# Ten of eleven FFN pairs as groups, first sums by transfer, and a tail by token tiles

## The chip, the cores and the metric

The kernel runs on one core of a Trainium2 chip. The metric is the device time of one execution in microseconds; the kernel before stands at 2078.82 us, the median of three runs (2076.89 to 2081.77).

## The reference

One layer of a macaron block on 256 tokens, model width 2048, in fp32: half a SwiGLU FFN, two token mixers side by side, a second half FFN and a last RMSNorm.

```python
x = x + 0.5 * swiglu_ffn(rmsnorm(x, norm_ffn1_g[l]), ffn1_w_gate[l], ffn1_w_up[l], ffn1_w_down[l])
h = rmsnorm(x, norm_mix_g[l])
proj = h @ w_in[l]
...
merged = jax.nn.sigmoid(gate_a) * branch_a + jax.nn.sigmoid(gate_r) * branch_r
x = x + merged @ w_out[l]
x = x + 0.5 * swiglu_ffn(rmsnorm(x, norm_ffn2_g[l]), ffn2_w_gate[l], ffn2_w_up[l], ffn2_w_down[l])
return rmsnorm(x, norm_final_g)
```

where `swiglu_ffn` is `(silu(x @ w_gate) * (x @ w_up)) @ w_down` with an inner width of 5632. branch_a is band attention over 8 heads with a clipped relative-position bias, branch_r is chunkwise retention over 8 heads.

## The kernel before

**One product.** Each fp32 operand is split into a high and a low part, and a product is three matmuls: high by high, low by high, high by low (L132, L133, L135; `three`). The weights are split on the fly: ACT copies a 128x1024 tile to the high part (L123), VectorE subtracts it from the raw tile for the low part (L124; `split`).

**Standard steps.** A `Gemm` has an output of 256 tokens by 512 columns in two PSUM banks. Its step takes 256 rows of the weight: a load by SP (L117), a split, and 12 matmuls of 128x512.

**Groups.** The inner width is 11 blocks of 512 columns. For each block the gate and the up product are needed: a *pair*. As two `Gemm`s a pair has 16 standard steps, 192 matmuls. As a *group* (class `Strassen`) the two products are built by seven block products in place of eight, 28 steps of six matmuls, 168 in all. Its phases, with jc = 0..3:
- phase 0, r: split of k[jc] (bank a); VectorE also makes the first sum x[jc] = x[jc] + k[jc] (L505). Phase 0, s: split of that x[jc] (bank c).
- phase 1, r: a raw weight tile, split (bank c); VectorE adds it to x[jc] (L560). Phase 1, s: split of x[jc] (bank a); VectorE makes k[jc] = x[jc] - k[jc] (L547), and an accumulating transfer on POOL adds another part of the up weight to x[jc] (L548, the third sum).
- phase 2, r: a raw tile (bank b). Phase 2, s: k[jc] (bank a). Phase 3, s: x[jc] (bank a).

r and s alternate, so 10r names phase 1, jc 0, r. Between phases a bank is read by ACT: a after 03r into b (L600), c after 03s (L603), a after 13s and after 23s (L617); VectorE joins the partial results (L733 and its neighbours), ACT applies silu. Then TensorE transposes the block (f1a4p is block 4 of FFN 1), and its halves are split for the down product (`put`, L353 and L354). The operands k and x of the next group are eight POOL loads of 512 KB (L516), each issued when a tile of an earlier group is free. The mixing stage has five groups of the same kind.

**The order.** An FFN makes some of the blocks as plain pairs (`PLAIN`) and the rest as groups. The down product runs in passes (`PASSES`), each over one or two blocks as four `Gemm`s, whose accumulators ACT seeds with the running sum (L750) and evicts to it (L753). `weave` writes the order of all steps down: it lays the group's steps in order and puts a standard step after a pair of them when a credit, fed by the table `SHARE`, allows and the standard step's blocks are at hand (`at_hand`, a fixed number of steps after the last step of the block). Preparation (load, split) runs up to four steps ahead of the products (four split buffers). `later(n)` puts work n steps further on.

**Tail.** The last down block's two steps (`TAIL` = 2) run by token tile and column part; the last norm's scaling and the stores of both token tiles stand at the end (`scale_rows`).

**The code.** The functions that the change touches, with the profile's line numbers:

Of the kernel before, what the change touches and what calls it, by code (L numbers as in the profile page):

```python
# [11 lines left out]
ALU = mybir.AluOpType  # L12
# [3 lines left out]
P = 128  # L16
SEQ = 256
NT = SEQ // P
# [14 lines left out]
SPLIT_BUFS = 4  # L33
KEPT = 8
ACT_TILES = 30
TAIL = 2
AHEAD = (2, 3)
HALF_K = D // P // 2
LEAD = 12
# [1 line left out]
RET_WAIT = (14, 5)  # L41
HELD = 6

SHARE = (0.85,) * 4 + (1.0,) * 4 + (0.8,) + (0.4,) * 3 + (0.15,) * 4
PLAIN = (9, 10)
PASSES = ((9, 0), (1, 2), (10, 3), (4, 5), (6,), (7,), (8,))
GATE_WAIT = 5
WARM = (6, 3)
TAIL_PARTS = ((0, slice(0, NB)), (1, slice(0, NB // 2)), (1, slice(NB // 2, NB)))

# [22 lines left out]
def block_kernel(ctx: ExitStack, tc: tile.TileContext, x, g1, w1g, w1u, w1d, gm, w_in, rel, woa, wor, wo,  # L73
# [156 lines left out]

    def run(tail_done):
        head = len(steps) - TAIL
        last = steps[-1].job
        last.parts = TAIL_PARTS
# [12 lines left out]
        for part, (t, cs) in enumerate(TAIL_PARTS):  # L247
            for c in range(head, len(steps)):
                steps[c].products(part)
            tail_done(last.acc[part], t, cs)  # L250
        while due:
            s = min(due)
            state["step"] = max(s, state["step"])
            for fn in due.pop(s):
                fn()
# [73 lines left out]
    def bias_natural(bt):  # L329
        for b in range(HEADS // 4):  # L330
            table["bias", b] = act_tile(F32, f"bias{b}")
        for h in range(0, HEADS, 2):
            ps = side_tile(f"psb{h}")
            for i in range(2):
                for j in range(2):
                    nc.tensor.transpose(
                        ps[:, (2 * i + j) * P : (2 * i + j + 1) * P],
                        bt[(h + i) // 4][:, (h + i) % 4, j * P : (j + 1) * P],
                        id_sb,
                    )  # L340
            nc.scalar.copy(table["bias", h // 4][:, h % 4 : h % 4 + 2, :].rearrange("p h k -> p (h k)"), ps)
        for b in range(HEADS // 4):
            nc.vector.memset(table["bias", b][0:CHUNK, :, CHUNK:P], MASKED)


    def rsqrt(dst, ssum, n, width):
# [143 lines left out]
    class Strassen:  # L490
# [19 lines left out]

        def loads(self):


            def go(tiles, i, jc):
                tiles[jc] = apool.tile([P, KC, NB], F32, tag="act", name=f"{self.name}{'kx'[i]}{jc}")
                nc.gpsimd.dma_start(tiles[jc], chunk(self.w[i], self.rows(0, jc), self.col[i]))  # L516

            return [
                lambda tiles=tiles, i=i, jc=jc: go(tiles, i, jc)
                for jc in range(HALF_K // KC) for i, tiles in enumerate((self.kept, self.x))  # L520
            ]

        def steps(self):
# [10 lines left out]
        def step(self, phase, jc, of_sum):  # L534
# [15 lines left out]
            def prep():  # L550
                x = self.x[jc]
                if not of_sum:
                    if phase == 0:
                        made["w"] = split(self.kept[jc], name)
                        self.first(jc)
                        return
                    raw = made.pop("raw")
                    made["w"] = split(raw, name)
                    if phase == 1:
                        nc.vector.tensor_add(x, x, raw)  # L560
                elif phase == 2:
# [85 lines left out]
    def weave(jobs, apart, groups, lead, start=None):  # L647
# [17 lines left out]

        for _ in range(lead):
# [4 lines left out]
        for n, (b, make) in enumerate(groups.items()):  # L671
# [15 lines left out]
    def ffn(name, norm, wg, wu, wd, after, start=None):  # L687
# [10 lines left out]
        def plain(b):  # L698
# [15 lines left out]
            def up_done(acc):  # L714
                for t in range(NT):
                    a = gates[t]
                    nc.vector.scalar_tensor_tensor(a, acc[t], norm.scale(t), a, op0=ALU.mult, op1=ALU.mult)  # L717
# [7 lines left out]
        def paired(b):  # L725
            got = {}

            def evict(t, side, r):
# [3 lines left out]
                    return  # L732
                nc.vector.scalar_tensor_tensor(got[t], r, norm.scale(t), got[t], op0=ALU.mult, op1=ALU.mult)  # L733
                if t == 1:
                    later(3, lambda: put_mid(b, got))

            return Strassen(norm, wu, b * NB, wg, b * NB, evict)

# [336 lines left out]
        for t in range(NT):  # L1075
            last_square(t, slice(b * NB, (b + 1) * NB), b)

    def tail_done(acc, t, cs):
        cols = slice(D - NB + cs.start, D - NB + cs.stop)
        xb = xs[t][:, cols]  # L1080
        part = D // NB - 1 + (cs.start > 0)
        if cs.stop == NB:
# [3 lines left out]
        nc.vector.scalar_tensor_tensor(xb, acc, 0.5, xb, op0=ALU.mult, op1=ALU.add)  # L1086
        if "end" not in fin:
            fin["end"] = tmp_tile(f"end{t}", "qk", 4)
        end = fin["end"]
        last_square(t, cols, part, end[:, cs])  # L1090
        if cs.stop < NB:
            return
        del fin["end"]
        v = small.tile([P, 1], F32, tag="v", name="v")
        nc.vector.tensor_scalar(v, nf_ss[:, t, part : part + 1], 1.0 / D, before, op0=ALU.mult, op1=ALU.add)
        rs = small.tile([P, 1], F32, tag="frs", name="frs")
        nc.gpsimd.tensor_tensor(rs, v, mhalf[:, :1], op=ALU.pow)
        fin[t] = rs, end

        if t == NT - 1:  # L1100
            for u in range(NT):
                scale_rows(u)

    def scale_rows(t):
        rs, end = fin[t]
# [137 lines left out]
```

## Time and profile before

| | |
|---|---|
| median of 3 runs | 2078.82 us (2076.89 to 2081.77) |
| profiled execution | 2078.51 us, its span 2076.4 us |
| TensorE busy | 2048.9 us, 99% of the span |
| VectorE busy | 1756.2 us, 85% |
| ScalarE busy | 1404.3 us, 68% |
| GpSimd busy | 273.7 us, 13% |
| chain that ended last | PE 92% |
| HBM read | 462.65 MB |

In the profile, PE is TensorE, DVE is VectorE, ACT is ScalarE, POOL is GpSimd, and SP issues the weight transfers. The chain is followed back from the last instruction: at each step to what released it. A name as `loz12823s` is the low part (`lo`) of the group that begins at step 128 (`z128`), phase 2, jc 3, s.

### The profile page before, as it was taken

To read this page: it belongs to the slowest core of one execution; us is meant where nothing else is said; L and a number is where in the kernel's file an instruction comes from. 1 tells how busy PE (TensorE), PEld (TensorE's weight loads), DVE (VectorE), ACT (ScalarE), POOL (GpSimd) and SP (SyncE) were. 2 spreads that over 40 slices of the span, in tenths; PEclk is the share of its full clock that TensorE was granted. 3 is DMA by queue.
4 is the path that set the end of the run, shared out by engine and by line. 5 is a ranking of instruction groups with operands and counts; after the bars stand their busy time and mean duration, and the time that the engine had idled before them with its cause. 6 is when DMAs were issued, how large, how long until landed. Compare 5 with 4: busy or idle time off the path is not lost.

```text
span 2076.4 us, 26151 instructions
## 1 busy us (share of the span) xinstructions
PE 2048.9 (99%) x9256; PEld 1692.5 (82%) x9256; DVE 1756.2 (85%) x1823; ACT 1404.3 (68%) x1734; POOL 273.7 (13%) x322
## 2 busy tenths in 40 slices
PE   9999999999999999999999999999999999999997
PEld 7788888888888888888878888888888878888886
DVE  7998899898997799898866667568889988998986
ACT  8677667777777776767665434556676677677785
POOL 1111211122111111112100000010122112210200
PEclk9999999999999999999999999999999999999999
DMA  8777886788678777789775645575788668866873
GB/s 305 210 223 232 263 238 197 239 256 260 189 229 263 242 209 242 252 273 281 226 243 173 222 137 189 186 248 165 236 270 244 187 228 264 248 197 233 274 213 132
DMA packets 219027, 473.28 MB, mean 228 GB/s; under 512 B 14784, under 2 KB 15536, under 8 KB 218896
## 3 DMA queue, kind: packets, MB, share of 16 engines
q1 hardware_dynamic: 161088, 310.42, 44.6%
q0 software_dynamic: 54752, 155.88, 27.8%
q10 hardware_dynamic: 3056, 5.32, 0.7%
q8 instruction: 72, 1.18, 0.2%
q14 instruction: 59, 0.48, 0.1%
HBM read 462.65 MB, written 8.91 MB: 227 GB/s over the span
## 4 chain that ended last, share of the span: by engine, by line
PE 92%; DVE 2%; DMA 2%; ACT 2%; issue 1%; ACTq 0%; POOLq 0%; DVEq 0%; POOL 0%
PE acc L132 17%; PE acc L135 17%; PE acc L133 17%; DMA raw<-in_ffn_w_down_dram 1%; DMA rawz53123r<-in_w_in_dram 1%; DVE lo L124 1%; ACT hi L123 0%; PE z128a L132 0%; PE z12a L135 0%; PE z128a L135 0%; PE z128a L133 0%; PE z12a L132 0%; PE z915a L135 0%; PE z418a L135 0%; PE z761a L132 0%
## 5 line engine op out<-in xcount | busy, mean ns | idle before, releaser
L124 DVE TENSOR_TENSOR lo<-raw,hi 128x1024 fp32r<-128x1024 f32 (+1 forms) x401 | 488.4, 1221 | 186.2 <-ACT hi L123 182.9
L123 ACT CAST hi<-raw 128x1024 fp32r<-128x1024 f32 (+1 forms) x401 | 418.7, 1048 | 231.1 <-PE acc L133 148.1
L753 ACT ACTIVATE xall<-acc 128x512 f32<-128x512 f32 x96 | 56.5, 589 | 9.4 <-PE acc L135 7.6
L750 ACT ACTIVATE acc<-xall 128x512 f32<-128x512 f32 x96 | 57.5, 599 | 8.0 <-DVE f2g L717 3.4
L132 PE MATMUL acc<-hi,mgh 128*128 128x512 f32 x128 | 50.2, 392 | 0.0
L133 PE MATMUL acc<-hi,mgl 128*128 128x512 f32 x128 | 49.8, 389 | 0.0
L132 PE MATMUL acc<-hi,nma00h 128*128 128x512 f32 x96 | 38.5, 401 | 0.0
L132 PE MATMUL acc<-hi,nma01h 128*128 128x512 f32 x96 | 38.4, 400 | 0.0
L133 PE MATMUL acc<-hi,nma00l 128*128 128x512 f32 x96 | 37.4, 390 | 0.0
L132 PE MATMUL acc<-hi,nma10h 128*128 128x512 f32 x96 | 37.4, 390 | 0.0
L133 PE MATMUL acc<-hi,nma01l 128*128 128x512 f32 x96 | 37.4, 390 | 0.0
L133 PE MATMUL acc<-hi,nma11l 128*128 128x512 f32 x96 | 37.4, 390 | 0.0
L133 PE MATMUL acc<-hi,nma10l 128*128 128x512 f32 x96 | 37.4, 389 | 0.0
L132 PE MATMUL acc<-hi,nma11h 128*128 128x512 f32 x96 | 37.4, 389 | 0.0
L135 PE MATMUL acc<-lo,mgh 128*128 128x512 f32 x128 | 35.5, 389 | 0.0
L135 PE MATMUL acc<-lo,nma11h 128*128 128x512 f32 x96 | 29.6, 390 | 0.0
L135 PE MATMUL acc<-lo,nma00h 128*128 128x512 f32 x96 | 29.6, 389 | 0.0
L135 PE MATMUL acc<-lo,nma01h 128*128 128x512 f32 x96 | 29.6, 389 | 0.0
L135 PE MATMUL acc<-lo,nma10h 128*128 128x512 f32 x96 | 29.6, 389 | 0.0
L135 PEld LDWEIGHTS acc<-lo,mgh 128*128 128x128 f32 x128 | 24.0, 188 | 5.0
L133 PEld LDWEIGHTS acc<-hi,mgl 128*128 128x128 f32 x128 | 24.0, 188 | 4.9
L132 PEld LDWEIGHTS acc<-hi,mgh 128*128 128x128 f32 x128 | 24.0, 188 | 4.8
(6130 smaller groups left out, 6934.6 us busy)
## 6 DMA issues: line engine op xcount, KB each, us to landing
raw<-in_ffn_w_down_dram SPq DMA_DIRECT2D x176, 512.0 KB, 6.2
raw<-in_w_in_dram SPq DMA_DIRECT2D x96, 512.0 KB, 4.4
raw<-in_ffn_w_up_dram SPq DMA_DIRECT2D x32, 512.0 KB, 10.0
raw<-in_w_out_dram SPq DMA_DIRECT2D x32, 512.0 KB, 4.4
raw<-in_ffn_w_gate_dram SPq DMA_DIRECT2D x31, 512.0 KB, 5.8
raw<-in_w_out_att_dram SPq DMA_DIRECT2D x16, 512.0 KB, 4.1
raw<-in_w_out_ret_dram SPq DMA_DIRECT2D x16, 512.0 KB, 3.8
z380x<-in_w_in_dram POOLq DMA_DIRECT2D x8, 512.0 KB, 7.5
```

Of the source, the lines that this page charges most:

```text
L123: nc.scalar.copy(hi[:, p, :], raw[:, p, :])
L124: nc.vector.tensor_sub(lo[:, p, :], raw[:, p, :], hi[:, p, :].bitcast(F32))
L132: nc.tensor.matmul(acc, ahi, whi, start=first, stop=False, **more)
L133: nc.tensor.matmul(acc, alo, whi, start=False, stop=False, **more)
L135: nc.tensor.matmul(acc, ahi, wlo, start=False, stop=last, **more)
L750: nc.scalar.activation(acc, xs[t][:, cols], AF.Copy, scale=2.0)
L753: nc.scalar.activation(xs[t][:, cols], acc, AF.Copy, scale=0.5)
```

## The change

1. One plain pair instead of two: block 9 alone is standard, block 10 becomes a group. The passes become (9), (0,1), (2,3), (4,5), (6,7), (8), (10); `SHARE`'s third and fourth entry go from 0.85 to 0.5; blocks count as at hand one step later; the transposes of a block come a step later (`later(4)`).
2. The first sums of jc 2 and 3 of every group are accumulating POOL transfers (`BY_VECTOR` = 2), issued behind the group's eight loads, in place of an add on VectorE.
3. The transposes of the bias before attention are four turns, one step apart, with the mask set in each turn.
4. The last two down blocks (four steps) run by token tile: token tile 0 of both blocks, then 1; scaling and stores of tile 0 stand before tile 1's products.

```diff
-SHARE = (0.85,) * 4 + (1.0,) * 4 + (0.8,) + (0.4,) * 3 + (0.15,) * 4
-PLAIN = (9, 10)
-PASSES = ((9, 0), (1, 2), (10, 3), (4, 5), (6,), (7,), (8,))
+SHARE = (0.85,) * 2 + (0.5,) * 2 + (1.0,) * 4 + (0.8,) + (0.4,) * 3 + (0.15,) * 4
+PLAIN = (9,)
+PASSES = ((9,), (0, 1), (2, 3), (4, 5), (6, 7), (8,), (10,))
+BY_VECTOR = 2
...
             def go(tiles, i, jc):
                 nc.gpsimd.dma_start(tiles[jc], chunk(self.w[i], self.rows(0, jc), self.col[i]))
+                if i == 1 and jc == n - 1:
+                    for j in range(BY_VECTOR, n):
+                        nc.gpsimd.dma_start(
+                            self.x[j], chunk(self.w[0], self.rows(0, j), self.col[0]), accum_op=ALU.add
+                        )
...
                         made["w"] = split(self.kept[jc], name)
-                        self.first(jc)
+                        if jc < BY_VECTOR:
+                            self.first(jc)
...
-                at_hand[job.makes] = len(steps) + 5
+                at_hand[job.makes] = len(steps) + 6
...
-                    at_hand[b] = len(steps) + 6
+                    at_hand[b] = len(steps) + 7
...
-                later(3, lambda: put_mid(b, gates))
+                later(4, lambda: put_mid(b, gates))
...
-        first, second = [plain(b) for b in PLAIN]
-        order = [first, second[:1], downs[PASSES[0]], second[1:]] + [downs[p] for p in PASSES[1:]]
+        order = [plain(b) for b in PLAIN] + [downs[p] for p in PASSES]
...
-        for h in range(0, HEADS, 2):
+        def turn(h):
...
+        turn(0)
+        for h in range(2, HEADS, 2):
+            later(h // 2, lambda h=h: turn(h))
...
-TAIL = 2
+TAIL = 4
...
-        for part, (t, cs) in enumerate(TAIL_PARTS):
-            for c in range(head, len(steps)):
-                steps[c].products(part)
-            tail_done(last.acc[part], t, cs)
+        for t in range(NT):
+            for job in ends:
+                for part, (u, cs) in enumerate(job.parts):
+                    if u == t:
+                        for c in range(head, len(steps)):
+                            if steps[c].job is job:
+                                steps[c].products(part)
+                        tail_done(job.acc[part], t, slice(job.col0 + cs.start, job.col0 + cs.stop))
```

What this does to the order on the engines, at three places. Each step of a group appears as one `lo` and one `hi` tile. On TensorE, the end of phase 2 of the third group of FFN 1 (z89) before; `acc_0` and `acc_1` are the banks of a standard step:

```order
L135 MATMUL z89a<-loz8923s,n1s7h 128x512 x2
L132 MATMUL acc_0_2062<-hi_2130,n1a01h 128x512
L133 MATMUL acc_0_2062<-hi_2130,n1a01l 128x512
L132 MATMUL acc_0_2062<-hi_2130,n1a01h 128x512
L133 MATMUL acc_0_2062<-hi_2130,n1a01l 128x512
L132 MATMUL acc_1_2063<-hi_2130,n1a11h 128x512
L133 MATMUL acc_1_2063<-hi_2130,n1a11l 128x512
L132 MATMUL acc_1_2063<-hi_2130,n1a11h 128x512
L133 MATMUL acc_1_2063<-hi_2130,n1a11l 128x512
L135 MATMUL acc_0_2062<-lo_2131,n1a01h 128x512 x2
L135 MATMUL acc_1_2063<-lo_2131,n1a11h 128x512 x2
L132 MATMUL z89a<-hiz8930s,n1a11h 128x512
```

and the end of phase 2 of the second group (z48) of the changed kernel, the lines being one further down:

```order
L133 MATMUL z48a<-hiz4823s,n1s7h 128x512
L134 MATMUL z48a<-hiz4823s,n1s7l 128x512
L133 MATMUL z48a<-hiz4823s,n1s7h 128x512
L134 MATMUL z48a<-hiz4823s,n1s7l 128x512
L136 MATMUL z48a<-loz4823s,n1s7h 128x512 x2
L133 MATMUL z48a<-hiz4830s,n1a11h 128x512
L134 MATMUL z48a<-hiz4830s,n1a11l 128x512
L133 MATMUL z48a<-hiz4830s,n1a11h 128x512
L134 MATMUL z48a<-hiz4830s,n1a11l 128x512
L136 MATMUL z48a<-loz4830s,n1a11h 128x512 x2
```

Before, a standard step of 12 matmuls stands between the last product of phase 2 and the first of phase 3, which both write bank a; in the changed kernel none does in this group. On VectorE, phase 1 of z128 before, from the split of 11s to that of 20r (`lo_` without z is a standard step's):

```order
L124 TENSOR_TENSOR loz12811s<-z128x_2122,hiz12811s 128x1024
L547 TENSOR_TENSOR z128k_2104<-z128x_2122,z128k_2104 128x1024
L124 TENSOR_TENSOR loz12813r<-rawz12813r,hiz12813r 128x1024
L560 TENSOR_TENSOR z128x_2191<-z128x_2191,rawz12813r 128x1024
L124 TENSOR_TENSOR lo_2493<-raw_2390,hi_2492 128x1024
L354 TENSOR_TENSOR f1a10l_2499<-f1a10p_2500,f1a10h_2498 128x4x128
L354 TENSOR_TENSOR f1a10l_2499<-f1a10p_2507,f1a10h_2498 128x4x128
L124 TENSOR_TENSOR loz12812s<-z128x_2158,hiz12812s 128x1024
L547 TENSOR_TENSOR z128k_2146<-z128x_2158,z128k_2146 128x1024
L124 TENSOR_TENSOR loz12813s<-z128x_2191,hiz12813s 128x1024
L547 TENSOR_TENSOR z128k_2173<-z128x_2191,z128k_2173 128x1024
L124 TENSOR_TENSOR lo_2551<-raw_2404,hi_2550 128x1024
```

and of z48 in the changed kernel (L564 is the subtraction, L578 the add):

```order
L125 TENSOR_TENSOR loz4811s<-z48x_958,hiz4811s 128x1024
L564 TENSOR_TENSOR z48k_946<-z48x_958,z48k_946 128x1024
L125 TENSOR_TENSOR loz4813r<-rawz4813r,hiz4813r 128x1024
L578 TENSOR_TENSOR z48x_1039<-z48x_1039,rawz4813r 128x1024
L125 TENSOR_TENSOR loz4812s<-z48x_1001,hiz4812s 128x1024
L564 TENSOR_TENSOR z48k_988<-z48x_1001,z48k_988 128x1024
L125 TENSOR_TENSOR loz4813s<-z48x_1039,hiz4813s 128x1024
L564 TENSOR_TENSOR z48k_1015<-z48x_1039,z48k_1015 128x1024
L125 TENSOR_TENSOR loz4820r<-rawz4820r,hiz4820r 128x1024
L125 TENSOR_TENSOR loz4821r<-rawz4821r,hiz4821r 128x1024
L125 TENSOR_TENSOR loz4820s<-z48k_854,hiz4820s 128x1024
L125 TENSOR_TENSOR loz4822r<-rawz4822r,hiz4822r 128x1024
```

The standard steps' splits and a block's put, which stood between those of phase 1, are absent from the stretch from 11s on. On POOL, the loads of a group's operands before (z128):

```order
L516 DMA z128k_2034<-in_ffn_w_up_dram 128x2x512
L516 DMA z128x_2080<-in_ffn_w_gate_dram 128x2x512
L516 DMA z128k_2104<-in_ffn_w_up_dram 128x2x512
L516 DMA z128x_2122<-in_ffn_w_gate_dram 128x2x512
L516 DMA z128k_2146<-in_ffn_w_up_dram 128x2x512
L516 DMA z128x_2158<-in_ffn_w_gate_dram 128x2x512
L516 DMA z128k_2173<-in_ffn_w_up_dram 128x2x512
L516 DMA z128x_2191<-in_ffn_w_gate_dram 128x2x512
L548 DMA z128x_2080<-in_ffn_w_up_dram 128x2x512
L548 DMA z128x_2122<-in_ffn_w_up_dram 128x2x512
```

and in the changed kernel (z80):

```order
L528 DMA z80k_1370<-in_ffn_w_up_dram 128x2x512
L528 DMA z80x_1396<-in_ffn_w_gate_dram 128x2x512
L528 DMA z80k_1422<-in_ffn_w_up_dram 128x2x512
L528 DMA z80x_1434<-in_ffn_w_gate_dram 128x2x512
L528 DMA z80k_1446<-in_ffn_w_up_dram 128x2x512
L528 DMA z80x_1458<-in_ffn_w_gate_dram 128x2x512
L528 DMA z80k_1470<-in_ffn_w_up_dram 128x2x512
L528 DMA z80x_1485<-in_ffn_w_gate_dram 128x2x512
L531 DMA z80x_1458<-in_ffn_w_up_dram 128x2x512
L531 DMA z80x_1485<-in_ffn_w_up_dram 128x2x512
L565 DMA z80x_1396<-in_ffn_w_up_dram 128x2x512
L565 DMA z80x_1434<-in_ffn_w_up_dram 128x2x512
```

Behind the eight loads stand two accumulating transfers (L531) of the first sums of jc 2 and 3; the third sums (L548 before, L565 now) follow.

More of the change, by code (lines that the diff above doesn't have):

```diff
@@ L232, in run @@
         head = len(steps) - TAIL
-        last = steps[-1].job
-        last.parts = TAIL_PARTS
+        ends = [steps[head].job, steps[-1].job]
+        ends[1].parts = TAIL_PARTS
         for c in range(head):
@@ L340, in bias_natural @@
                     )
-            nc.scalar.copy(table["bias", h // 4][:, h % 4 : h % 4 + 2, :].rearrange("p h k -> p (h k)"), ps)
-        for b in range(HEADS // 4):
-            nc.vector.memset(table["bias", b][0:CHUNK, :, CHUNK:P], MASKED)
+            dst = table["bias", h // 4][:, h % 4 : h % 4 + 2, :]
+            nc.scalar.copy(dst.rearrange("p h k -> p (h k)"), ps)
+            nc.vector.memset(dst[0:CHUNK, :, CHUNK:P], MASKED)
+        turn(0)
+        for h in range(2, HEADS, 2):
+            later(h // 2, lambda h=h: turn(h))
     def rsqrt(dst, ssum, n, width):
@@ L511, in loads @@
         def loads(self):
+            n = HALF_K // KC
             def go(tiles, i, jc):
@@ L516, in go @@
                 nc.gpsimd.dma_start(tiles[jc], chunk(self.w[i], self.rows(0, jc), self.col[i]))
+                if i == 1 and jc == n - 1:
[3 more added lines that the diff above has]
+                        )
             return [
                 lambda tiles=tiles, i=i, jc=jc: go(tiles, i, jc)
-                for jc in range(HALF_K // KC) for i, tiles in enumerate((self.kept, self.x))
+                for jc in range(n) for i, tiles in enumerate((self.kept, self.x))
             ]
@@ L734, in evict @@
                 if t == 1:
-                    later(3, lambda: put_mid(b, got))
+                    later(4, lambda: put_mid(b, got))
             return Strassen(norm, wu, b * NB, wg, b * NB, evict)
@@ L1076, in last_block, with tail_done @@
             last_square(t, slice(b * NB, (b + 1) * NB), b)
-    def tail_done(acc, t, cs):
-        cols = slice(D - NB + cs.start, D - NB + cs.stop)
+    def tail_done(acc, t, cols):
         xb = xs[t][:, cols]
-        part = D // NB - 1 + (cs.start > 0)
-        if cs.stop == NB:
+        part = cols.start // NB + (cols.start % NB > 0)
+        if cols.stop == D:
             before = small.tile([P, 1], F32, tag="ftot", name="ftot")
@@ L1086, in tail_done @@
         nc.vector.scalar_tensor_tensor(xb, acc, 0.5, xb, op0=ALU.mult, op1=ALU.add)
+        if cols.start < D - NB:
+            last_square(t, cols, part)
+            return
         if "end" not in fin:
@@ L1089, in tail_done @@
         end = fin["end"]
-        last_square(t, cols, part, end[:, cs])
-        if cs.stop < NB:
+        last_square(t, cols, part, end[:, cols.start - (D - NB) : cols.stop - (D - NB)])
+        if cols.stop < D:
             return
@@ L1097, in tail_done @@
         nc.gpsimd.tensor_tensor(rs, v, mhalf[:, :1], op=ALU.pow)
[L1098 to L1105, printed above, removed]
         rows = slice(t * P, (t + 1) * P)
```

## The prediction

> **What bounds the kernel now.** I read the engine totals first, then the chain of waits, then what TensorE waited for, and last the stretches. The profiled execution took 2078.51 us, span 2076.4 and 2.1 us around it; the median of the three runs is 2078.82, 0.3 higher. The sum below is made against 2078.5.
>
> ```profile
> PE 2048.9 (99%) x9256; PEld 1692.5 (82%) x9256; DVE 1756.2 (85%) x1823; ACT 1404.3 (68%) x1734; POOL 273.7 (13%) x322
> PE 92%; DVE 2%; DMA 2%; ACT 2%; issue 1%; ACTq 0%; POOLq 0%; DVEq 0%; POOL 0%
> ```
>
> TensorE is busy for 99% of the span and makes 92% of the chain, so time is saved by fewer matmuls or by fewer waits of TensorE. This is the list of its waits (total, times, longest, in us):
>
> ```profile
> PE f1a9p L359 <- DVE f1g L717: 2.3, 1, 2.3
> PE psb L336 <- ACT bias L341: 2.1, 1, 2.1
> ...
> PE acc L132 <- ACT hi L123: 1.2, 2, 1.0
> PE f1a4p L359 <- DVE z166c L733: 0.8, 1, 0.8
> PE f2a4p L359 <- DVE z838c L733: 0.8, 1, 0.8
> PE z877a L132 <- ACT z877c L617: 0.8, 1, 0.8
> PE z128a L132 <- ACT z128c L617: 0.8, 1, 0.8
> ...
> PE f2a0p L359 <- DVE z684c L733: 0.3, 1, 0.3
> ```
>
> All of these are short; z205a, z380a and z800a stand there too with the same 0.8. The kernel has little slack to give, but also little reserve: an engine that falls behind adds its time directly. VectorE has stretches without any idle time, and the transfers are full in others (us; busy by engine; then clock, DMA share, GB/s):
>
> ```profile
> 180.00:208.00 28.00, 28.00 (x130) 23.26 (x129) 27.89 (x27) 21.01 (x26) 0.22 (x1) 1.00 0.41 128
> 208.00:250.00 42.00, 42.00 (x187) 34.80 (x186) 36.79 (x35) 27.42 (x30) 10.47 (x12) 1.00 1.02 314
> 250.00:272.00 22.00, 22.00 (x103) 18.31 (x102) 22.00 (x22) 15.63 (x17) 0.00 (x0) 1.00 0.35 104
> ```
>
> In one group's period (some 68 us) VectorE is full in phases 0 and early 1, where DMA stands at 0.35 to 0.41; DMA is full in the 42 us of the third sums, the standard weights and the next group's loads. The clock is 1.00 throughout.
>
> **The tenth pair as a group.** Two group steps of six matmuls start 1.36 us apart, 0.227 us a matmul:
>
> ```profile
> 1669.20 0.39 PE L132 MATMUL z800a<-hiz80021s,n2s7h 128*128 128x512 f32 x1
> 1670.56 0.39 PE L132 MATMUL z800b<-hiz80023r,n2a01h 128*128 128x512 f32 x1
> ```
>
> A standard pair has 192 matmuls, a group 168. Two FFNs save 48: 48 x 0.227 = **-10.9 us**. This lies wholly on TensorE's path. Sixteen SP loads go; 16 POOL loads, 8 more third sums and 50 first sums by transfer come.
>
> **Bank waits.** With one plain pair only, each standard step must wait for a pass of two, so groups alternate between 4 or 5 and 11 or 12 standard steps, where each had 10 or 11. Where no standard step lies between a group's last product of phase 2 and the first of phase 3, the bank must first be read by ACT:
>
> ```profile
> 310.68 0.61 PE L135 MATMUL z128a<-loz12823s,n1s7h 128*128 128x512 f32 x2
> 312.07 0.50 PE L132 MATMUL z128a<-hiz12830s,n1a11h 128*128 128x512 f32 x1 [0.78 <-ACT z128c L617]
> ...
> 311.33 0.69 ACT z128c L617
> ...
> 268.91 0.69 ACT L603 ACTIVATE z128s<-z128c,n1minus 128x512 f32<-128x512 f32 x1 [0.76 <-PE z128c L135]
> ```
>
> The x2 row takes two spacings (0.45), so TensorE was due at 311.13 and went on at 312.07: 0.94 us. In the program's order such direct neighbours rise from 5 to 9 groups: +3.8. The same happens to bank c between phases 0 and 1 in 3 groups (48, 543, 732, named by the step at which they begin in the changed program) where it happened in none; ACT reads it there by L603, a scaled copy of 0.69 like L617's, so 3 x 0.94 = +2.8. Together **+6.6**. Bounds: 0 if VectorE is behind there anyway and the waits coincide, 8 if the c bank's costs 1.3.
>
> **VectorE.** These rows show its prices and its lead:
>
> ```profile
> 183.44 1.22 DVE L505 TENSOR_TENSOR z89x<-z89x,z89k 128x1024 f32<-128x1024 f32 x1
> 184.57 1.22 DVE L124 TENSOR_TENSOR lo<-raw,hi 128x1024 fp32r<-128x1024 f32 x1
> 186.84 0.75 DVE L733 SCALAR_TENSOR_TENSOR z51c<-z51a,n1rstd,z51c 128x512 f32<-128x512 f32 x1
> 187.50 1.22 DVE L124 TENSOR_TENSOR loz8902r<-z89k,hiz8902r 128x1024 fp32r<-128x1024 f32 x1
> ...
> 258.55 1.28 DVE L354 TENSOR_TENSOR f1a2l<-f1a2p,f1a2h 128x512 fp32r<-128x512 f32 x2
> 259.74 1.22 DVE L124 TENSOR_TENSOR loz12803r<-z128k,hiz12803r 128x1024 fp32r<-128x1024 f32 x1
> ...
> 266.55 1.22 DVE L124 TENSOR_TENSOR loz12810r<-rawz12810r,hiz12810r 128x1024 fp32r<-128x1024 f32 x1
> 272.33 0.62 PE L135 MATMUL z128c<-loz12810r,n1s3h 128*128 128x512 f32 x2
> ```
>
> Back to back, a split or sum costs 1.135 us, an eviction 0.66 and the two halves of a put 1.19. The low half of 10r is done at 267.77 and used at 272.33: a lead of 4.56 us, about as long as four prepared steps allow. Two first sums of four per group leave VectorE (92 become 50: 42 x 1.135 = 47.7 us), and 24 splits, 8 more adds and 8 more subtractions come (45.4): the total hardly moves. But where it falls does. Eight phase-1 steps cost VectorE 16 x 1.135 = 18.2 us and TensorE 10.9; each standard step gives back 2.72 - 1.135 = 1.58.
>
> In FFN2's first group phase 1 now holds one standard step, before three. VectorE 19.3 against TensorE 13.6: 5.7 behind, less the lead of 4.56, 1.1; with two evictions (L717) ahead of the transposes, part of which waits already, I take +1.7. In FFN1 the same place already loses 2.3 (f1a9p above), I take +0.6. In the transitions from an early to a late group, 20 to 24 group steps run without a standard step. Phase 1 with two standard steps costs 20.4 against 16.3, within the lead and 0.5 left; phases 2 and 3 give 12 x (1.36 - 1.135) less two evictions, +1.4; the next phase 0 costs 8 splits, 2 adds, 2 evictions and sometimes a third and a put (12.7 to 14.5) against 10.9, -1.8 to -3.6. So such a transition ends between level and 1.7 us behind; a bank wait of 0.94 in it gives VectorE that time. I take 0.5 for four of them (+2.0) and nothing for the others. The put now comes a step later, which takes 1.4 off the 1.9 us of f1a4p, f2a4p and f2a0p. Together **+2.9**; bounds -2 (the first sums' relief carries everything) and +18 (rival two).
>
> **Transfers.** What a first sum by transfer costs, from the page's queues and issues:
>
> ```profile
> q1 hardware_dynamic: 161088, 310.42, 44.6%
> q0 software_dynamic: 54752, 155.88, 27.8%
> ...
> z128x<-in_ffn_w_gate_dram POOLq DMA_DIRECT2D x4, 512.0 KB, 11.6
> z128x<-in_ffn_w_up_dram POOLq DMA_DIRECT2D x4, 512.0 KB, 6.4
> ```
>
> And these from the timeline, the last load of a group's operands and the use of its sum:
>
> ```profile
> 238.89 0.72 POOL L516 DMA_DIRECT2D z128x<-in_ffn_w_gate_dram  x1 [0.41 <-DVE loz8923s L124]
> 262.21 1.05 ACT L123 CAST hiz12803s<-z128x 128x1024 fp32r<-128x1024 f32 x1 [1.31 <-DVE z128x L505]
> 264.28 1.22 DVE L124 TENSOR_TENSOR loz12803s<-z128x,hiz12803s 128x1024 fp32r<-128x1024 f32 x1
> 268.25 0.62 PE L135 MATMUL z128c<-loz12803s,n1s5h 128*128 128x512 f32 x2
> ```
>
> Over the trace SP issues 585 weight loads; its queue took 0.446 x 2076 = 926 us of the sixteen engines, 1.58 each. POOL's took 577 for 184 loads and 92 accumulating transfers; with loads at 1.58 an accumulating one takes 3.1. So two in a group take 6.2 us, after the full 42 and in a stretch at 0.35 to 0.41: there is room. In time: the last load was issued at 238.89, lands about 11.6 later at 250.5, and an accumulating transfer takes 6.4 to land: 256.9, 5.3 before ACT needs the sum at 262.21. Four standard steps stand between the two; where they are gone the need comes 10.9 earlier and SP's four loads (6.3) go as well, so the sum would be 5.3 - 10.9 + 6.3 = 0.7 early, or 5.6 late if the loads land no sooner. Its low half is done at 265.50 and used at 268.25, so a lead of 2.75 covers part of that. I take **+1.4** in all, between 0 and the third rival.
>
> [...]
>
> **The small edits.** The bias transposes in four turns, each a standard step apart, let ACT read a bank behind 2.72 us of matmuls: **-2.1**. The wait for hi at 1671.7 was a late SP weight, at a place that is now arranged otherwise: **-1.1** (bounds 0 and -1.2; a new one elsewhere would be like it). The tail:
>
> ```profile
> 2065.59 0.40 PE L135 MATMUL acc<-lo,f2a8h 128*128 128x256 f32 x2
> 2067.07 0.71 ACT L1110 ACTIVATE xall<-xall,frs 128x512 f32<-128x512 f32 x1
> ...
> 2067.49 0.99 POOL L1097 TENSOR_TENSOR frs<-v,mhalf 128x1 f32<-128x1 f32 x1 [1.92 <-DVE v L1095]
> ...
> 2069.14 0.71 ACT L1110 ACTIVATE end<-end,frs 128x512 f32<-128x512 f32 x1
> ...
> 2070.91 0.61 SPq L1111 DMA_DIRECT2D out_dram<-end  x1
> ```
>
> The matmuls end 10 us before the span does. Six stores of 2.1 MB go out behind them; now the first token tile's three are issued about when the matmuls end. The second's chain (square, power, scale, issue) still runs from the last matmul, and the work of two blocks is queued ahead of it on ACT and VectorE, about 1 us. The last store ends 5.5 us after its issue at 2070.91, behind the bytes of the others; with half of them gone I estimate 2 us less of that, and 1 us more of chain: **-0.9** (bounds -2.5 and +0.5).
>
> **Sum.** -10.9 + 6.6 + 2.9 + 1.4 - 2.1 - 1.1 - 0.9 = -4.1; 2078.5 - 4.1 = **2074.4 us**. What a measurement can tell from no change is about 0.2%, 4.2 us, so this lies at the edge of faster (below 2074.7) and same.
>
> **The rivals.**
> - *The new waits do not come.* VectorE is relieved of first sums where it was full (22.00 of 22), so the transitions cost nothing and half of the bank waits fall under late low halves: -10.9 + 3.3 - 1.4 (puts) - 4.1 (small edits) = -13.1; with the transfers' 1.4 and 1.1 of FFN2's first group about **2068**. For it: VectorE's total does not grow. Against: the bank waits need only a direct neighbour, and those are counted.
> - *VectorE becomes the bound in the runs without standard steps.* Eight transitions lose 0.9 to 1.7, the worse half of the span above, and the two first groups 4.5: 7.2 + 4.5 = 11.7 to 13.6 + 4.5 = 18.1 in place of 2.9, so 2083 to 2090, in the middle **2086**. For it: full stretches of VectorE before. Against: two adds less just there. It decides once the lead at phase 1's start is under 3 us.
> - *The accumulating transfers land late*, slower than before. Eight transitions, each 5.6 late less a lead of 2.75, are 8 x 2.9 = 23 in place of 1.4: **2096**. For it: the full 42 us; against: the four SP loads that go with the standard steps. It decides once the last load still takes 11.6 us to land.
>
> **Chances.** Forecast 0.45 (own range 2071 to 2079), no new waits 0.23, VectorE 0.20, transfers 0.12. Faster: 0.23 and a little over half of the forecast's, 0.48. Same (to 2083): the rest of the forecast's and a third of VectorE's, 0.28. Slower: the rest of VectorE's and the transfers, 0.24. The range 2066 to 2087 leaves out the transfers' case and the ends of two others.
>
> **What would show it.** 48 matmuls of 128x512 fewer; ACT's copies out of banks a and c releasing TensorE 12 times, 0.94 us each; f2a9p waiting 1 to 2 us; psb gone from the waits; the first tile's stores issued by the end of the matmuls. ACT's hi of 02s and 03s waiting for a transfer would speak for the third rival; many waits of TensorE for low halves after group 48, 120, 191 and 263 for the second. The forecast is wrong if neither shows and the bank waits are fewer than eight, or if TensorE's idle time in the transitions passes 10 us.

## The result: 3.5% slower, and the profile after

The changed kernel takes 2153.15 us (median of 4 runs, 2149.97 to 2154.83) against 2078.24 for the kernel before: a ratio of 1.0354, 95% interval 1.0338 to 1.0370. The prediction was 2074.4 with a range of 2066 to 2087. (Of all the executions timed here one, of e10, took 9036 us; it is left out of e10's ratio.) The profiled execution has a span of 2151.9 us, 75.5 more than before. Engine totals of the changed kernel:

```profile
PE 2076.2 (96%) x9208; PEld 1683.9 (78%) x9208; DVE 1758.0 (82%) x1827; ACT 1425.3 (66%) x1766; POOL 354.6 (16%) x396
```

TensorE has 48 matmuls fewer, as forecast, and VectorE's busy time moved by 2 us. But TensorE, 99% before, is at 96%, and its busy time rose with fewer matmuls, for two reasons given in the last section. What TensorE waited for (total, times, longest):

```profile
PE acc L133 <- ACT hi L124: 10.3, 7, 1.9
PE acc L136 <- DVE lo L125: 8.3, 17, 0.6
PE z764c L133 <- ACT hiz76402s L124: 2.9, 1, 2.9
PE z908c L133 <- ACT hiz90802s L124: 2.8, 1, 2.8
...
PE f1a10p L370 <- DVE gains L281: 2.2, 1, 2.2
PE z224c L133 <- ACT hiz22402s L124: 2.0, 1, 2.0
...
PE z120a L133 <- ACT z120c L635: 0.9, 1, 0.9
...
PE z48c L133 <- ACT z48s L621: 0.8, 1, 0.8
...
PE f2a9p L370 <- DVE f2g L735: 0.4, 1, 0.4
```

The waits for the high halves of 02s and 03s, in bank c of one group after the other, were in no row before; the bank waits (z120a, z48c) are those that the prediction counted. To see all of it, I took from the trace each gap between the starts of two matmuls of 512 columns, subtracted 0.227 us, and summed what exceeded 0.06 us by the operand of the matmul that came late (matmuls that ran at a slower clock, 0.54 from 176.5 to 184, are in these rows too, some 8 us in all):

| TensorE late for | before, us | changed, us |
|---|---|---|
| high half of 0s (first sums) | 1.4 | 30.5 |
| low half of 0s | 0 | 10.5 |
| low half of a standard step | 1.2 | 18.6 |
| high half of a standard step | 8.3 | 24.1 |
| low half of 2r | 0.5 | 3.5 |
| bank a before 30s | 5.2 | 10.5 |
| bank c before 10r | 0.1 | 3.3 |
| transposes of the bias (psb) | 2.1 | 0 |
| all gaps, small ones too | 34.4 | 121.5 |

121.5 - 34.4 = 87.1; less 10.9 for the matmuls and 0.5 for the tail this is 75.7, the 75.5 of the span. By groups, the loss lies in the eight late groups: 8 to 10 us at each of z80, z152, z224, z296 and z764, z836, z908, z980, each just behind 20 to 24 group steps without a standard step, and 1 to 5 at each of the other FFN groups.

One such transition, z48 to z80. POOL first (its columns: start, duration, operation, and the idle time before it with what ended it):

```profile
147.37 1.19 POOL L565 DMA_DIRECT2D z48x<-in_ffn_w_up_dram  x1 [1.05 <-DVE z48k L564]
148.10 1.23 POOL L528 DMA_DIRECT2D z80k<-in_ffn_w_up_dram  x1
...
158.16 0.72 POOL L528 DMA_DIRECT2D z80x<-in_ffn_w_gate_dram  x1 [3.27 <-DMA z48x<-in_ffn_w_up_dram]
169.55 1.24 POOL L531 DMA_DIRECT2D z80x<-in_ffn_w_up_dram  x1 [10.67 <-DMA z80x<-in_ffn_w_gate_dram]
172.16 1.21 POOL L531 DMA_DIRECT2D z80x<-in_ffn_w_up_dram  x1 [1.38 <-DMA z80x<-in_ffn_w_gate_dram]
```

Then ACT, which makes the high halves:

```profile
175.60 1.04 ACT L124 CAST hiz8002s<-z80x 128x1024 fp32r<-128x1024 f32 x1 [3.89 <-DMA z80x<-in_ffn_w_up_dram]
178.79 1.04 ACT L124 CAST hiz8003s<-z80x 128x1024 fp32r<-128x1024 f32 x1 [2.15 <-DMA z80x<-in_ffn_w_up_dram]
```

And the stretches (us; busy by engine; clock, DMA share, GB/s):

```profile
150.00:158.00 8.00, 8.00 (x37) 6.54 (x35) 7.50 (x8) 5.57 (x7) 3.68 (x6) 1.00 1.08 306
158.00:169.00 11.00, 9.97 (x43) 7.72 (x42) 10.66 (x11) 6.58 (x8) 0.72 (x1) 1.00 1.03 390
169.00:184.00 15.00, 12.49 (x44) 8.72 (x44) 9.51 (x10) 8.49 (x11) 2.45 (x2) 0.77 0.49 91
```

The last third sum of z48 is issued at 147.37, six of the next group's eight loads right behind it, and the last two at 154.16 and 158.16, after waits of 1.2 and 3.3 us. DMA is full until 169. The last load takes 13.7 us to land (158.16 to 171.87 in the trace; in the eight late groups 13.0 to 15.5), others up to 17.5. POOL waits 10.67 us for the load under the first sum, and the two sums take 6.0 and 6.5 us more to land; ACT stands 3.89 and 2.15 us for them. Meanwhile VectorE is nearly full too (10.66 of 11): two resources run out in the same window. In 169 to 184 TensorE has 44 matmuls where 66 would fit, and the granted clock is 0.77.

VectorE's lead, from the end of a low half to its use on TensorE, was spent before that, in phase 1 of z48. The low halves of 10r and of 20r:

```profile
125.47 1.23 DVE L125 TENSOR_TENSOR loz4810r<-rawz4810r,hiz4810r 128x1024 fp32r<-128x1024 f32 x1 [0.34 <-ACT hiz4810r L124]
131.15 0.62 PE L136 MATMUL z48c<-loz4810r,n1s3h 128*128 128x512 f32 x2
...
146.74 1.22 DVE L125 TENSOR_TENSOR loz4820r<-rawz4820r,hiz4820r 128x1024 fp32r<-128x1024 f32 x1
148.01 0.73 PE L136 MATMUL z48b<-loz4820r,n1a01h 128*128 128x512 f32 x2 [0.37 <-DVE loz4820r L125]
```

4.45 us of lead at the start of phase 1 are 0.05 at the start of phase 2, and TensorE waits.

### The profile page after: what moved, and what is told of

The parts are those of the page before. It is cut to its first block, busy times and chain, and to the rows that moved or that the text cites. A ratio compares the mean times of both kernels' runs of the same rounds, so it can differ in the third digit from the quotient of the medians.

```text
span 2151.9 us, 26219 instructions
## 1 busy us (share of the span) xinstructions
PE 2076.2 (96%) x9208; PEld 1683.9 (78%) x9208; DVE 1758.0 (82%) x1827; ACT 1425.3 (66%) x1766; POOL 354.6 (16%) x396
## 5 line engine op out<-in xcount | busy, mean ns | idle before, releaser
L125 DVE TENSOR_TENSOR lo<-raw,hi 128x1024 fp32r<-128x1024 f32 (+1 forms) x369 | 448.4, 1219 | 202.1 <-ACT hi L124 200.1
L124 ACT CAST hi<-raw 128x1024 fp32r<-128x1024 f32 (+1 forms) x369 | 385.3, 1048 | 240.0 <-PE acc L134 144.5
L133 PE MATMUL acc<-hi,nma00h 128*128 128x512 f32 x96 | 38.6, 402 | 0.0
L134 PEld LDWEIGHTS acc<-hi,mgl 128*128 128x128 f32 x128 | 24.1, 188 | 4.8
```

The source lines that it names most:

```text
L124: nc.scalar.copy(hi[:, p, :], raw[:, p, :])
L125: nc.vector.tensor_sub(lo[:, p, :], raw[:, p, :], hi[:, p, :].bitcast(F32))
L133: nc.tensor.matmul(acc, ahi, whi, start=first, stop=False, **more)
L134: nc.tensor.matmul(acc, alo, whi, start=False, stop=False, **more)
```

## The experiments

The questions: is it the first sums by transfer, the long runs without standard steps, or the tenth group itself? Times are medians beside the kernel before on the same chip. The new SHARE and the two shifts by a step (`at_hand` and `later`) were not run alone; they count here as part of the order.

| kernel | order | groups per FFN | first sums 2, 3 | us | ratio, interval |
|---|---|---|---|---|---|
| before | even | 9 | VectorE | 2078 to 2080 | 1 |
| e2 | even | 9 | transfer | 2078.45 | 0.9998 (0.9989 to 1.0007) |
| e4 | even, small edits | 9 | VectorE | 2076.18 | 0.9985 (0.9976 to 0.9994) |
| e10 | even, small edits | 9 | transfer | 2073.81 | 0.9977 (0.9967 to 0.9986) |
| e5 | uneven | 9 | VectorE | 2100.93 | 1.0103 (1.0083 to 1.0124) |
| e6 | uneven | 9 | transfer | 2117.24 | 1.0182 (1.0159 to 1.0204) |
| changed | uneven | 10 | transfer | 2153.15 | 1.0354 (1.0338 to 1.0370) |
| e1 | uneven | 10 | VectorE | 2132.97 | 1.0261 (1.0241 to 1.0281) |
| e3 | claim held at 1 | 10 | transfer | 2095.39 | 1.0080 (1.0066 to 1.0093) |
| e7 | claim held at 1 | 10 | VectorE | 2102.51 | 1.0111 (1.0094 to 1.0128) |
| e8 | even, short passes | 10 | transfer | 2089.83 | 1.0049 (1.0034 to 1.0065) |
| e11 | as e8 | 10 | transfer, 1 to 3 | 2132.27 | 1.0254 (1.0240 to 1.0268) |

### e1: first sums back on VectorE

```diff
-BY_VECTOR = 2
+BY_VECTOR = 4
```

> The changed kernel with all four first sums of a group on VectorE again (BY_VECTOR = 4); order of steps, small edits and all else as changed. Theory A (the two first sums by transfer land late where 20 to 24 group steps run without a standard step): the waits of TensorE for the high halves of 02s and 03s, about 30 us of the changed kernel, go, and with them the weight waits and slow matmuls behind them; VectorE is two adds slower in each phase 0, 2 x 1.135 x 8 = 18 at the most. Time 2095 to 2115. Theory B (the long runs without standard steps cost by themselves, since VectorE and the operand loads have no cover; the transfers only give the wait its name): the wait moves to the low halves and to the k tiles, 2140 to 2165.

2132.97 us: 20 of the 75 come back. The waits for high halves of 0s fall from 30.5 to 0.7, as theory A said, but 53 us remain, with low halves (22.3 before standard steps, 7.9 in 0s, 4.3 in 2r), late weights (19.6) and the banks (13 waits of 0.8 to 0.9). Neither theory had it alone: A named the wait that vanished, B was nearer in time.

### e2: the transfers alone, in the order of before

```diff
                 nc.gpsimd.dma_start(tiles[jc], chunk(self.w[i], self.rows(0, jc), self.col[i]))
+                if i == 1 and jc == n - 1:
+                    for j in range(BY_VECTOR, n):
+                        nc.gpsimd.dma_start(
+                            self.x[j], chunk(self.w[0], self.rows(0, j), self.col[0]), accum_op=ALU.add
+                        )
...
-                        self.first(jc)
+                        if jc < BY_VECTOR:
+                            self.first(jc)
```

> The kernel before with only the first sums of jc 2 and 3 moved to accumulating transfers; two plain pairs, 10 or 11 standard steps in every group. Theory A (late only where standard steps are missing): 2074 to 2082, no wait for the high halves of 02s and 03s above 1 us in sum. Rival (an accumulating transfer behind the loads is late in every group, 2 us or more): 24 x 2 = 48, 2120 or more.

2078.45 against 2079.56: no difference. With 10 or 11 standard steps in each group the transfers land in time everywhere, TensorE waits 1.4 us for high halves of 0s as before, and the 46 sums taken from VectorE gain nothing that can be told from the noise.

### e3 and e7: the claim held at 1

A group that finds no standard step at hand goes on collecting credit, and the next one spends it in a burst. With the credit held at 1, the groups from the fourth on have 7 or 8 standard steps.

```diff
-                credit += rate * SHARE[i]
+                credit = min(credit + rate * SHARE[i], 1.0)
```

> The changed kernel with the credit of the order's planner held at 1 at the most, so that a group that could place no standard step does not hand its claim to the next: from the third group on 6 to 8 standard steps in every group and runs of at most 8 (20 in one transition), in place of 4 and 12 by turns. Theories A and B: most of the 75 us go, 2075 to 2090, one or two late transitions left. Rival (8 standard steps a group are too few for VectorE and the transfers, however they lie): 2110 or more.

2095.39, 58 us below the changed kernel by the order alone. That was near the theories' 2075 to 2090 but not in it. The largest loss left is at z80 and z764, 8 us each, where a run of 20 group steps remains. e7 is the same with BY_VECTOR = 4:

> The changed kernel with the claim for standard steps held at 1 and all first sums on VectorE. If VectorE is what 7 or 8 standard steps a group run into, the low halves come later than with transfers: 2100 to 2115 against 2095. If the 8 us lost at each of the groups 80 and 764 are the transfers' lateness, 2080 to 2090.

2102.51: the first of its cases. Low halves of standard steps are 17.5 us late where e3 had 12.1. The second case is in it too: at z80 and z764 the loss falls from 8 us to 4. So with the claim held at 1 the transfers help (by 7 us in all); in the uneven order they hurt (by 20, e1).

### e4: the small edits alone

Items 3 and 4 of the change, on the kernel before:

```diff
-TAIL = 2
+TAIL = 4
...
-        for h in range(0, HEADS, 2):
+        def turn(h):
...
+        turn(0)
+        for h in range(2, HEADS, 2):
+            later(h // 2, lambda h=h: turn(h))
```

> The kernel before with only the two small edits: bias transposes in four turns and the last two down blocks by token tile. Forecast of the prediction: -2.1 and -0.9, 2075.2 where before stands at 2078.2. Rival (the tail loses what the bias gains, since the work of two blocks is queued ahead of the last scaling): no change, 2078.

2076.18, 3.4 us less by medians, interval 1.2 to 5.0 us. In its trace psb is gone from the waits, and the last matmul starts at 2064.2 in place of 2065.7. From there the span's end is 10.1 us away, before 10.7: the tail gains 0.6.

### e5 and e6: only the order made uneven

```diff
+                bare = len(groups) > 5 and (n % 2 == 1 and i >= 8 or n % 2 == 0 and 0 < n and i < 3)
+                if bare:
+                    continue
                 if credit >= (0.2 if (i + 1) % (HALF_K // KC) == 0 else 0.6) and next_standard():
```

> The kernel before (two plain pairs, all first sums on VectorE), with nothing changed but where the standard steps lie: none in phases 2 and 3 of every second FFN group and in three quarters of phase 0 of the next, so that in eight transitions 20 group steps run without one, and groups hold 7 or 8 and 13 by turns. Theory B (such runs cost by themselves): 8 x 5 = 40 more, 2110 to 2125. Theory A (only first sums by transfer make them costly): the bank waits, four more of 0.94, and little else, 2080 to 2087.

2100.93: 21 us for nothing but where the standard steps lie, between the two theories' ranges. Its waits of TensorE:

```profile
PE f2a5p L359 <- DVE z876c L736: 1.7, 1, 1.7
PE f1a5p L359 <- DVE z204c L736: 1.7, 1, 1.7
PE f2a3p L359 <- DVE z799c L736: 1.5, 1, 1.5
```

Each of the eight transitions ends with the transposes of a block waiting 1.5 to 1.7 us for VectorE's last eviction: 12.8 us by the gaps, where before only f1a4p and f2a4p had 0.8 each. Bank waits add 4.2 and low halves of standard steps 4.2. No wait for a high half of 0s is above 1.5 us.

> The same uneven order on the kernel before, with the first sums of jc 2 and 3 by accumulating transfer. Where the even order showed no difference between the two ways (2078.45 against 2079.56), here: if lateness of the transfers needs a run without standard steps, 15 to 30 us above the uneven order with sums on VectorE, with waits for the high halves of 02s and 03s; if not, the same as that or, by the relief of VectorE, 5 to 10 below.

2117.24: 16 us more, the first of the cases. With e2 this is the clearest result of the study. The same two transfers per group cost -1 us in the even order and +16 in the uneven one:

```profile
PE z240c L133 <- ACT hiz24003s L124: 2.8, 1, 2.8
PE z989c L133 <- ACT hiz98902s L124: 2.8, 1, 2.8
```

The waits of the transposes are mostly gone (none for a block's is above 1.2 us; VectorE is relieved), and 23.8 us of waits for high halves of 0s have come in their place.

### e8: ten groups in an even order, and e9: VectorE relieved there

```diff
-PASSES = ((9,), (0, 1), (2, 3), (4, 5), (6, 7), (8,), (10,))
+PASSES = ((9,), (0,), (1,), (2,), (3,), (4, 5), (6, 7), (8,), (10,))
...
-                credit += rate * SHARE[i]
+                credit = min(credit + rate * SHARE[i], 1.0 if len(groups) > 5 else 99)
```

> The changed kernel with the claim held at 1 in the FFNs and down passes over one block each for blocks 0 to 3, so that a standard step is at hand in the third and fourth group too: 6 to 8 in every group, no run above 12. If evenness is what counts: the 16 us of groups 80 and 764 go, 2075 to 2083. Rival (the seeds and evictions of two more passes on ACT cost as much): 2090 or more.

2089.83, between the two cases. The transitions no longer stand out (0 to 5 us a group), and yet it is 10 us over before with 48 matmuls fewer: evenness was not all. In e9 the subtraction is left out:

```diff
-                nc.vector.tensor_sub(k, x, k)
```

> The kernel with even claims and short passes (2089.83), its subtraction k = x - k in phase 1 left out, four operations of 1.135 us on VectorE in each group; the seventh product then uses the old k, so the output is another. Nothing else changes, but that the third sums can start as soon as x is split. If VectorE is what bounds ten groups: the waits for low halves (16 us before standard steps, 4.4 in 1s, 3.3 in 0s) go, 2062 to 2072. If the transfers or the banks bound it: 2085 or more.

2060.06 (ratio 0.9909, 0.9892 to 0.9927), 30 us below e8, and 2 below what I had expected at the least. What bounds ten groups in an even order is VectorE: low halves came 27 us late in e8 and 5.5 in e9, while the high halves of standard steps, which would show late weights, go only from 9.1 to 7.9. So it is not the earlier third sums that gave the 30 us. One row of the waits of TensorE, of e8:

```profile
PE acc L136 <- DVE lo L125: 9.2, 16, 0.6
```

and of e9:

```profile
PE acc L136 <- DVE lo L125: 1.1, 2, 0.6
```

### e10: all of the change but the tenth group and its order

> The kernel before (two plain pairs, its own order) with the two small edits and the first sums of jc 2 and 3 by transfer, so all of the change but the tenth group and the order that goes with it. Small edits alone gave 2076.2, transfers alone 2078.5: 2074 to 2076.5 if they add up; 2079 if the relief of VectorE and the edits do not.

The edits of e2 and e4 together: 2073.81 us, the fastest of the kernels that leave nothing out, 0.23% under before (interval 0.14 to 0.33) and just below its first case. Whether the transfers give a little here is not shown: e10 is 2.4 us below e4 by medians and 1.7 by the ratios, whose intervals overlap.

### e11: a third first sum by transfer

```diff
-BY_VECTOR = 2
+BY_VECTOR = 1
```

> The kernel with even claims and short passes, with three first sums by transfer (BY_VECTOR = 1). VectorE has 1.135 us less in each of 20 FFN groups and the transfers 3.1 us more. If VectorE bounds it and transfers have room: 5 to 15 below 2089.8. If the transfers are late here too: 2095 or more, with waits for the high halves of 01s.

2132.27, 42 us over e8 and in the second case. VectorE was relieved and it was no use: high halves of 0s are 14.3 us late, and the waits for low halves of standard steps are 10.7 us, in e8 9.2. Three transfers do not fit where two do:

```profile
PE z1013c L133 <- ACT hiz101301s L124: 3.2, 1, 3.2
```

### e12, e13, e14: what the uneven order costs without first sums by transfer

From e1 (2132.97), e12 leaves out VectorE's subtraction, e13 the third sum's transfer, e14 both.

```diff
-                nc.vector.tensor_sub(k, x, k)
-                nc.gpsimd.dma_start(x, chunk(self.w[0], self.rows(1, jc), self.col[0]), accum_op=ALU.add)
```

> The changed kernel with all first sums on VectorE (2132.97) and, as in the run before, the subtraction k = x - k left out: four operations less on VectorE in each group, the output another, the uneven order and every transfer kept. If VectorE's lag is what the uneven order costs once the transfers' share is gone: the waits for low halves (22 us before standard steps, 8 in 0s, 4 in 2r) fall and the time is 2075 to 2095, with the 12 bank waits left. If late weights and operands behind the compressed transitions are: 2110 or more.

> The changed kernel with all first sums on VectorE (2132.97), its third sums' accumulating transfers left out (four of 512 KB in each group; phase 3 then uses another x, so the output is another), VectorE's work kept. If full transfers are a second cost of the uneven order beside VectorE: weights before standard steps are no longer late (12 us above the even order) and operands land earlier, 2110 to 2122, VectorE's waits for low halves still there. If VectorE alone decides while it has its full work: 2128 to 2133.

> The same with both the subtraction on VectorE and the third sum's transfer left out. With the subtraction alone left out the time was 2113.0 and weights were late by 22 us more than before. If those two, VectorE and the transfers, are what the uneven order costs beside its 12 bank waits: 2074 to 2090. If something else in the uneven order costs (banks, ACT): 2100 or more.

| | transfer kept | transfer left out |
|---|---|---|
| subtraction kept | 2132.97 | 2114.41 |
| subtraction left out | 2113.00 | 2087.09 |

e12 was expected at 2095 or less if VectorE was all; it came to 2113.0, its second case. That is the middle of two executions 10 us apart (2107.84 and 2118.17; the trace is of the longer), so its interval is wide: 1.0092 to 1.0226. Low halves of standard steps fall from 22.3 to 12.1 us, but the high halves go from 19.6 to 30.6: weights are later. ACT's waits for weights of the down product, in e1 and then in e12:

```profile
ACT hi L124 <- DMA raw<-in_ffn_w_down_dram: 37.7, 21, 3.1
...
ACT hi L124 <- DMA raw<-in_ffn_w_down_dram: 50.8, 29, 2.8
```

The changed kernel, with first sums by transfer, had this:

```profile
ACT hi L124 <- DMA raw<-in_ffn_w_down_dram: 43.8, 25, 3.6
```

Before it was 24.7, 15 times. In e13, without the third sums' transfers, it is nearly gone:

```profile
ACT hi L124 <- DMA raw<-in_ffn_w_down_dram: 1.0, 1, 1.0
```

e13 and e14 came in the first of their cases. So the late weights are the transfers' share, and half of the late low halves (38.6 us in e1, 20.2 in e12) go with the one subtraction of VectorE. Either relief alone gives 19 or 20, both 46. By the medians that is more than the sum, as if each of the two let the other bind when it is relieved; but with e12's two executions the one relief is 15 or 25, so that the excess, 2 to 12 us, is not well measured. Nor does e12 tell VectorE's relief from the third sums that start earlier with it. In e14 the bank waits are still there (z48a, z48c and their like, 12.8 us with those before), and some low halves (7.9 before standard steps, 5.4 in 0s). With less work than the kernel before it is still 8 us slower: the order's bank waits and the rest of the low halves.

## Point by point: why the prediction was wrong

- **48 matmuls, -10.9.** The count is right, 9208 in place of 9256, and the balance of the gaps above closes with it. The product of count and spacing held.
- **Bank waits, +6.6.** Right in place and size: twelve, 0.8 to 0.9 each by the waits; 5.3 + 3.2 = 8.5 by the gaps, just above the upper bound of 8 (seven of the twelve are new).
- **VectorE, +2.9.** The step that priced a transition "between level and 1.7 us behind" failed. It treated VectorE's lead of 4.56 us at the start of phase 1, read from one group, as full at each transition. In the trace of the changed kernel that lead is 3.4 to 4.5 us in the eight early groups of the transitions and 1.8 to 2.8 in the eight late ones; by 20r six of the early groups have 0.1 or 0.2 left, and at 00s of the late groups it is 0.1 to 0.5 (before, 1.5 at least), there with operands late as well. The second rival's condition, a lead under 3 us, thus held in all late groups. Low halves cost 10.5 + 18.6 + 3.5 - 1.7 = 31 us more than before, and e9 shows that even evenly laid out, with 6 to 8 standard steps to a group in place of 10 or 11, four operations of VectorE in each group decide over 30 us. I compared VectorE's total before and after and found it unchanged; but each standard step lends 1.58 us of cover and each group lost about three. This loss of cover has no term in the sum.
- **Transfers, +1.4.** The mechanism was the third rival's, to which I gave 0.12. e1 prices it at 20 us and e6 at 16; the rival said 23. The step that failed is the allowance that with the standard steps "SP's four loads (6.3) go as well", so that the last load would land sooner. It took 13.7 us in the transition quoted and 13.0 to 15.5 in all eight, longer than the 11.6 I had started from. The 11.6 was a median of four loads, too: the very load that I read, issued at 238.89, landed at 248.12, after 9.2. Third sums and eight loads were pushed into a shorter window, and the third sums are transfers of 3.1 us of the sixteen engines (the prediction's estimate) as well. DMA stood at 1.08 and 1.03 in the transition quoted (150 to 169), and SP's weights were late too: high halves of standard steps took 24.1 - 8.3 = 15.8 us more of TensorE's time, some 3 of it by the slower clock. No term or rival of the prediction had a price for that.
- **The rivals as alternatives.** I gave VectorE and the transfers as two cases with one outcome each, and in both took the same lead off the loss. They came together in one window (e12 to e14). Their prices from the prediction, 15 above the forecast's term for the far end of VectorE and 22 for the transfers, make 2111 with the forecast; the rest to 2153 I put down to late weights, the average loss of cover, and a slower clock (0.992 in the mean, before 0.999); no run splits it.
- **Bias, -2.1; wait at 1671, -1.1; tail, -0.9.** The first is right: psb is gone. The tail gave 0.5 (10.7 us from the last matmul's start to the end, then 10.2), and the first tile's stores were issued by 2141.1, ahead of the last matmul at 2141.7, as foreseen. e4 measured the two together at 3.4, interval 1.2 to 5.0, against 3.0 expected. The wait at 1671 went, and seven of its kind came (10.3 us in the waits above).
- **f2a9p, 1 to 2 us.** It waited 0.4; the gaps of that whole group come to 2.5 us against 0.5 before, half of them for low halves, so that the 1.7 taken for this place was about right. Not foreseen: f1a10p, 2.2 us behind VectorE's copy of the gains, since block 10's transposes now lie where the gains are turned.

## What to carry to other kernels

A unit of work that serves as cover is worth its engine balance, not its length: count, for each stretch, what the scarce engines and the transfers get from it, and price a run without it as one window in which all of them must finish. A lead (prepared steps, an early load) can be spent once. And when an order comes from claims that accumulate, look at what happens to a claim that can't be served: holding it (e3) was worth 58 us here.

## What the hardware showed that I had not expected

After some of the late sums, and once after a late weight (2022.79), TensorE ran at about half its rate for several microseconds. In the changed kernel at z80 (start, duration, operation):

```profile
176.69 0.50 PE L133 MATMUL z80c<-hiz8002s,n1s5h 128*128 128x512 f32 x1 [1.80 <-ACT hiz8002s L124]
...
180.91 0.63 PE L133 MATMUL z80c<-hiz8003s,n1s5h 128*128 128x512 f32 x1
181.33 0.63 PE L134 MATMUL z80c<-hiz8003s,n1s5l 128*128 128x512 f32 x1
...
185.09 0.40 PE L133 MATMUL acc<-hi,f1a0h 128*128 128x512 f32 x1
185.32 0.39 PE L134 MATMUL acc<-hi,f1a0l 128*128 128x512 f32 x1
```

The stretch around them, in the columns used above:

```profile
176.50:184.00 7.50, 6.67 (x16) 4.65 (x17) 5.36 (x6) 5.35 (x8) 0.00 (x0) 0.54 0.17 31
```

The spacing is 0.42 us in place of 0.23, the granted clock 0.54. Some forty matmuls of the changed kernel ran so, 0.2 us more each, some 8 us in six places; the kernel before and e1, without the late sums, have no such place between their first microseconds and their last matmul (mean granted clock 0.999 in both, 0.992 in the changed kernel). This is the smaller part of why TensorE's busy time rose with fewer matmuls. The larger part is how the profile draws a matmul: 0.39 us long, though the next starts 0.227 after it, so that up to 0.16 us of each late start counts as busy. Starts more than 0.06 us late were 352, before 122.

The slow clock set in at 177, 440, 1583, 1713, 1846 and 2024 us, and it didn't follow each gap: after 2.2 us at 437.6 it came, after 2.1 us at 568.9 not. The stretches of these two (us; TensorE busy; clock, DMA share, GB/s):

```profile
437.00:447.00 10.00, 7.50 (x24) 0.83 0.42 73
...
568.00:578.00 10.00, 6.70 (x24) 1.00 0.44 77
```

Behind the first, eight matmuls took 3.57 us (440.03 to 443.60) where 8 x 0.227 = 1.82 would do. So that stall cost 2.2 + 1.75, some 4 us. What decides whether the slow clock follows a gap is not shown here.
